# A decoder trunk on one core: three converted weight buffers and six raw ones in place of two and seven

## The chip, the cores and the metric

The kernel runs on one core of one Trainium2 chip. Its time is device microseconds (us) of one execution; the time of a kernel is the median over its runs. A core has TensorE (PE in the profile; PEld are its weight loads, which run beside the matmuls), VectorE (DVE), ScalarE (ACT) and GpSimd (POOL), each with a queue of its own that is worked off in order, and SyncE (SP), which here only issues DMAs.

## The reference

Two layers over 272 tokens (16 meta tokens and 256 of the sequence). Each layer mixes tokens (an RG-LRU group and an attention group side by side) and then adds PEER, a retrieval over 16384 experts of one neuron each:

```python
def peer(h, wq, subkeys, u, v):
    q = (h @ wq).reshape(B, T, PEER_HEADS, 2, D_SUBKEY)
    s = jnp.einsum('bthpd,pkd->bthpk', q, subkeys)
    top_s, top_i = lax.top_k(s, PEER_TOPK)
    ...
    gates = jax.nn.softmax(best_s, axis=-1)
    def one_chunk(args):
        hc, ec, gc = args
        act = gelu(einsum('cd,ckd->ck', hc, take(u, ec)))
        return einsum('ck,ckd->cd', gc * act, take(v, ec))

def reference(...):
    for l in range(2):
        z = rms_norm(h, mix_norm_g[l]) @ w_in[l]
        ...
        h = h + mixed @ w_out[l]
        h = h + peer(rms_norm(h, ffn_norm_g[l]), peer_wq[l], peer_subkeys[l], peer_u[l], peer_v[l])
    return h[:, N_META:]
```

## The kernel before

Most tokens do not gather their experts. For 224 tokens in layer 0 and 208 in layer 1 the kernel multiplies with all 16384 rows of `u`, applies the gelu, multiplies with a dense matrix of gates (zero but for the chosen experts) and multiplies with all rows of `v`. The other tokens fetch their rows one by one: a *gather* is one indirect DMA of 128 rows (512 KB), and a layer has 96.

All weights are fp32 and come as *blocks* of 128x1024 (512 KB). The list `order` fixes their sequence, per layer 14 of `w_in`, 8 of `w_out`, 16 of `wq`, 128 of `uT` (the u stage), 128 of `v` (the v stage), with the gathers put in between: 17 and 32 in the u stages of the two layers, 79 and 64 in the v stages. In the v stage of layer 1 one gather comes after every second block. Block loads are issued by SP (L147), gathers by POOL (L1067).

A load goes into one of the PF buffers of the pool `raw`, blocks and gathers in turn, so that load n reuses the buffer of load n-PF. Since TensorE multiplies in fp16, each block is split into a high half, `hi` (ScalarE, L216), and a rest, `lo` (VectorE, L217); `hi` and `lo` have two buffers each, which come free when TensorE has used them. A block is then 24 matmuls: 16 with `hi`, then 8 with `lo` (`mm3`, and L1142 for `v`). `block(kind, l, b)` is called before a block's matmuls: it has `conv` emit the split of the block after it, and the steps of the gathers in between. A gather is not split; VectorE works on it in the raw buffer (L1050 for `u`, a dot product; L1052 and L1054 for `v`, the sum `acc`), which frees the buffer.

In the v stage the activations are split as well, for two blocks at a time (`wsplit`): ScalarE writes the high part of `ww` (L1129), VectorE the rest (L1130). `ww` has two such pair buffers, and a pair is split one pair ahead.

In the `wq` and u stages VectorE also has the selection of the experts (top-k, one-hots, gates), which generators emit piece by piece between blocks. What stands where in an engine's queue is decided by a scheduler from the order of emission, from what is free by its own reckoning, and from a priority that the split has (`PRI`).

Of the kernel before, what the change touches and what calls it, by code (L numbers as in the profile page):

```python
# [10 lines left out]
F16 = mybir.dt.float16  # L11
# [15 lines left out]
NK = 128  # L27
# [19 lines left out]
NSP = (32, 48)  # L47
NU = (2, 2)
UB = (((64, 127, 16), (116, 124, 1)), ((60, 127, 32),))
PF = 7  # L50
ATT = ((3, 7), (1, 7))
LRU_AT = (1, 2, 3, 4)
LRU_FIRST = 0
# [88 lines left out]
def trunk(tc, a, out, dbg=None):  # L142
# [15 lines left out]
    with ExitStack() as ctx:  # L158
        per = ctx.enter_context(tc.tile_pool(name="per", bufs=1))
        raw_p = ctx.enter_context(tc.tile_pool(name="raw", bufs=PF))  # L160
        hl_p = ctx.enter_context(tc.tile_pool(name="hl", bufs=2))
        psp = ctx.enter_context(tc.tile_pool(name="psp", bufs=2, space=PSUM))
        PB = {"u": 2, "g": 2, "v": 4}

        def ps(tag):
            return psp.tile([128, 512], F32, name="ps_" + tag, tag=tag, bufs=PB[tag])
# [26 lines left out]
        def issue(n):  # L193
            while st["dma"] < min(n, len(order)):
                w, l, b = order[st["dma"]]
                t = raw_p.tile([128, D], F32, name="raw", tag="raw")
                if w == "gather":
                    hook["load"](t, *b)
                else:
                    dma(t, a[w][l, b])  # L200
                raws[st["dma"]] = t
                st["dma"] += 1

        def conv(n):
            while st["conv"] < min(n, len(order)):
                k = st["conv"]
                issue(k + PF)
                r = raws.pop(k)
                st["conv"] += 1
                if order[k][0] == "gather":  # L210
                    hook["step"](r, *order[k][2])
                    continue
                hi = hl_p.tile([128, D], F16, name="hi", tag="hi")
                lo = hl_p.tile([128, D], F16, name="lo", tag="lo")
                with tc.high_priority(offset=PRI):
                    A.activation(hi, r, AF.Copy, scale=WS)  # L216
                    V.scalar_tensor_tensor(out=lo, in0=r, scalar=WS, in1=hi, op0=ALU.mult, op1=ALU.subtract)  # L217
                hls[k] = (hi, lo)

        def ahead(k, n):  # L220
            while n:
                k += 1
                if k < len(order) and order[k][0] != "gather":
                    n -= 1
                elif k >= len(order):
                    break
            return k

        def block(kind, l, b):
            k = st["k"]  # L230
            while order[k][0] == "gather":
                k += 1
            assert order[k] == (kind, l, b), (order[k], kind, l, b)
            st["k"] = k + 1
            conv(ahead(k, 1) + 1)
            return hls.pop(k)

        def mm3(o, w, xhi, xlo, first=True, n=8, off=0):
# [19 lines left out]
        def area(tag, dt, shape=None, name=None):  # L258
            return per.tile(shape or [128, 8, T], dt, name=name or tag, tag=tag)
# [54 lines left out]
        def mixing(l, col, hh, hl, sq):  # L314
            SQ_H = [(one, sq[:, c]) for c in range(8)]
            C0 = NM if l else 0
            with tc.tile_pool(name="mix", bufs=1) as mp:
# [51 lines left out]
                def w_in(b):  # L369
                    w = block("w_in", l, b)  # L370
                    c0 = C0 if b >= 7 else 0
                    o = ps("v")[:, c0:T]
                    mm3(o, w, hh[:, :, c0:], hl[:, :, c0:])
                    return o
# [256 lines left out]
                def w_out_half(b, half, then=None):  # L631
                    w = block("w_out", l, 4 * half + b)
                    for m in range(2):
                        o = ps("u" if half else "v")[:, C0:T]
                        mm3(o, w, mh[:, 4 * half:, C0:], ml[:, 4 * half:, C0:], n=4, off=4 * m)
                        V.scalar_tensor_tensor(out=hT[:, 2 * b + m, C0:], in0=o, scalar=1.0 / WS, in1=hT[:, 2 * b + m, C0:], op0=ALU.mult, op1=ALU.add)
                        if then:
                            then(2 * b + m)
                        yield
# [112 lines left out]
                for b in range(4):  # L752
                    for _ in w_out_half(b, 1, then):
                        pass
                w = block("wq", l, 0)
                o = ps("v")[:, C0:T]
                mm3(o, w, hh[:, :, C0:], hl[:, :, C0:])
# [61 lines left out]
        def peer(l, col, hh, hl, rs, wq0):  # L819
            with tc.tile_pool(name="peer", bufs=1) as pp:  # L820
                SD = S - NSP[l]
# [9 lines left out]
                def al(shape, dt):  # L831
                    n = int(np.prod(shape))
                    e = n // 2 if dt == F16 else n
                    r = flata[:, cur[0]:cur[0] + e]
                    cur[0] += (e + 7) // 8 * 8
                    assert cur[0] <= cur_end[0]
                    if dt != F32:
                        r = r.bitcast(dt)
                    if len(shape) == 1:
                        return r  # L840
                    nm = "abcd"[:len(shape)]
                    return r.rearrange("p (%s) -> p %s" % (" ".join(nm), " ".join(nm)), **{nm[i]: shape[i] for i in range(len(shape) - 1)})
# [17 lines left out]
                hn = al([2, T], F32)  # L860
# [261 lines left out]
                    pump(PUMP[1] - prog["t"] / 960.0)  # L1122
                drain()
                pv = [ps("v") for _ in range(4)]
                ww = area("hn", F16, [128, 2, 2, 2, SD], "ww")

                def wsplit(j):
                    b = j // 2 % 2
                    A.activation(ww[:, b, 0], act[:, j:j + 2], AF.Copy)  # L1129
                    V.tensor_tensor(out=ww[:, b, 1], in0=act[:, j:j + 2], in1=ww[:, b, 0], op=ALU.subtract)  # L1130

                wsplit(0)
                for j in range(NK):
                    hi, lo = block("v", l, j)
                    if j % 2 and j + 1 < NK:
                        wsplit(j + 1)
                    wh, wl = ww[:, j // 2 % 2, 0, j % 2], ww[:, j // 2 % 2, 1, j % 2]

                    def mv(c, k):
                        o = pv[c // 2][:, (c % 2) * SD:(c % 2) * SD + SD]  # L1140
                        s = slice(c * 128, c * 128 + 128)
                        P.matmul(o, (hi, hi, lo)[k][:, s], (wh, wl, wh)[k], start=j == 0 and k == 0 and c % 2 == 0, stop=j == NK - 1 and k == 2, skip_group_check=True)  # L1142

                    if j < NK - 1:
                        for k in range(3):
                            for c in range(8):
                                mv(c, k)
                    else:
                        for c in range(8):
                            for k in range(3):  # L1150
                                mv(c, k)
                return pv

        if True:
# [12 lines left out]
            hh, hl = hx[:, 0], hx[:, 1]  # L1167
# [4 lines left out]
            for l in range(L):  # L1172
                hh, hl, rs, wq0 = mixing(l, cols[l], hh, hl, sq)
                if dbg is not None:
                    dma(dbg["h%d" % l], hT)
                pv = peer(l, cols[l], hh, hl, rs, wq0)
                if l + 1 < L:
                    hx, sq = area("gx", F16, [128, 2, 8, T], "hgx"), area("gy", F32)
                    hh, hl = hx[:, 0], hx[:, 1]
                for c in range(8):  # L1180
                    sd = S - NSP[l]
                    hd = hT[:, c, NM:NM + sd]
                    V.scalar_tensor_tensor(out=hd, in0=pv[c // 2][:, (c % 2) * sd:(c % 2) * sd + sd], scalar=1.0 / WS, in1=hd, op0=ALU.mult, op1=ALU.add)  # L1183
                    if l + 1 < L:
                        hsplit(c, cols[l + 1][:, C_MIX + c:C_MIX + c + 1], hh, hl, sq)
                    elif c % 2:
                        dma(out[:, c - 1:c + 1], hT[:, c - 1:c + 1, NM:T])


def build(arrays, dbg=False):  # L1190
    import concourse.bacc as bacc
    nc = bacc.Bacc("TRN2", target_bir_lowering=False, num_devices=1)
    aps = {k: nc.dram_tensor(k, v.shape, F32, kind="ExternalInput").ap() for k, v in arrays.items()}
    out = nc.dram_tensor("outT", (128, 8, S), F32, kind="ExternalOutput").ap()
    d = {"h%d" % l: nc.dram_tensor("h%d" % l, (128, 8, T), F32, kind="ExternalOutput").ap() for l in range(L)} if dbg else None
    with tile.TileContext(nc) as tc:
        trunk(tc, aps, out, d)
    return nc
# [9 lines left out]
```

## Time and profile before

| | |
|---|---|
| time, median of 3 runs | 1669.47 us (1664.43 to 1669.9) |
| the profiled execution | 1668.44 us, span 1666.7 us |
| PE busy | 1588.0 us, 95% of the span |
| PEld busy | 1467.8 us, 88% |
| DVE busy | 1503.8 us, 90% |
| ACT busy | 1098.2 us, 66% |
| POOL busy | 320.6 us, 19% |
| from HBM | 417.46 MB, 253 GB/s in the mean of all traffic |
| granted clock of TensorE | 0.993 of full speed |

The span is what the rows lie in; the execution's own time is 1.7 us longer. Matmuls overlap in the records, so a gap between them (idle time with its releaser in brackets) tells more than the busy share. DMA share is the mean busy share of the 16 DMA engines.

### The profile page before, as it was taken

The page shows a single profiled execution, that of the slowest core. Times are in us where ns is not written, and L with a number is a line of the kernel's source. Part 1 is how long each engine was busy: PE and PEld are TensorE (multiplying, and loading weights), DVE is VectorE, ACT ScalarE, POOL GpSimd, SP SyncE. Part 2 cuts the span into 40 slices and gives each one's busy share as a digit, 9 for nine tenths or more (in the row PEclk, how much of TensorE's full clock was granted, in tenths as well). Part 3 has the DMA queues.
Part 4 walks back from the last instruction along what each step waited for, and adds up shares of the span by engine and source line. Part 5 has one row for each costly group of instructions (what it writes and reads, how often), then busy time and mean ns, then how long its engine had stood idle before and what let it go on. Part 6 is the DMA issues. An engine that isn't in the chain of part 4 may idle for free.

```text
span 1666.7 us, 40245 instructions
## 1 busy us (share of the span) xinstructions
PE 1588.0 (95%) x15926; PEld 1467.8 (88%) x15926; DVE 1503.8 (90%) x3074; ACT 1098.2 (66%) x2001; POOL 320.6 (19%) x256
## 2 busy tenths in 40 slices
PE   9989999999999999999999899899999999999997
PEld 6667798899999999999967687789988899999997
DVE  6889989889999999988978899997999998989886
ACT  6857565789987555555557565678988755555653
POOL 1000000101102333333210000002124124353253
PEclk9999999999999999999999999999999999999999
DMA  7305465667777999999973054567787899999995
GB/s 291 114 11 169 141 208 198 216 204 235 246 257 254 339 374 360 367 358 352 359 260 119 3 178 140 201 217 237 229 278 272 279 351 333 346 353 353 365 338 203
DMA packets 117709, 421.21 MB, mean 253 GB/s; under 512 B 14416, under 2 KB 15824, under 8 KB 117008
## 3 DMA queue, kind: packets, MB, share of 16 engines
q1 hardware_dynamic: 88592, 317.88, 54.2%
q0 software_dynamic: 28928, 100.76, 17.4%
q8 instruction: 124, 2.03, 0.5%
q14 instruction: 65, 0.53, 0.1%
HBM read 417.46 MB, written 1.05 MB: 251 GB/s over the span
## 4 chain that ended last, share of the span: by engine, by line
PE 40%; DVE 14%; DMA 5%; ACT 3%; issue 3%; POOL 1%; DVEq 0%; POOLq 0%; ACTq 0%
PE ps_v L1142 26%; DVE lo L217 6%; PE ps_u L246 3%; DMA raw<-v,act 3%; PE ps_u L242 3%; PE ps_u L243 3%; ACT hi L216 1%; PE ps_g L966 1%; DMA raw<-v 1%; POOL raw L1067 1%; DVE act L767 1%; DVE act L764 1%; PE ps_v L243 1%; PE ps_v L242 1%; PE ps_v L246 1%
## 5 line engine op out<-in xcount | busy, mean ns | idle before, releaser
L216 ACT ACTIVATE hi<-raw 128x1024 f16<-128x1024 f32 x588 | 619.8, 1055 | 430.8 <-PE ps_v L1142 208.6
L217 DVE SCALAR_TENSOR_TENSOR lo<-raw,hi 128x1024 f16<-128x1024 f32 x588 | 710.6, 1218 | 71.2 <-ACT hi L216 64.0
L1142 PE MATMUL ps_v<-ww,hi 128*128 128x224 f16 (+1 forms) x4096 | 426.8, 257 | 11.0 <-DVE ww L1130 10.1
L242 PE MATMUL ps_u<-hn,hi 128*128 128x224 f16 (+2 forms) x2112 | 413.1, 257 | 8.2 <-ACT hi L216 6.8
L243 PE MATMUL ps_u<-hn,hi 128*128 128x224 f16 (+2 forms) x2112 | 413.0, 256 | 0.0
L1142 PEld LDWEIGHTS <-hi 128*128 128x128 f16 x4096 | 382.5, 98 | 13.6 <-issue 12.5
L246 PEld LDWEIGHTS <-lo 128*128 128x128 f16 x2656 | 244.1, 98 | 54.0 <-DVE lo L217 43.2
L242 PEld LDWEIGHTS <-hi 128*128 128x128 f16 x2656 | 260.0, 98 | 27.5 <-ACT hi L216 11.5
L243 PEld LDWEIGHTS <-hi 128*128 128x128 f16 x2656 | 259.9, 98 | 14.8 <-issue 4.5
L246 PE MATMUL ps_u<-hn,lo 128*128 128x224 f16 (+2 forms) x2112 | 242.0, 257 | 25.4 <-DVE lo L217 24.7
L1142 PE MATMUL ps_v<-ww,lo 128*128 128x224 f16 (+1 forms) x2048 | 235.7, 257 | 5.4 <-DVE lo L217 5.0
L1067 POOL DMA_INDIRECT raw<-ur,act x96 | 131.2, 1367 | 467.6 <-DVE lo L217 237.4
L1067 POOL DMA_INDIRECT raw<-v,act x96 | 157.8, 1644 | 248.1 <-DVE lo L217 186.4
L1142 PEld LDWEIGHTS <-lo 128*128 128x128 f16 x2048 | 190.5, 98 | 10.8 <-DVE lo L217 10.0
L957 ACT ACTIVATE ohb<-oha,gl 128x128 f16<-128x128 f16 x432 | 138.7, 396 | 13.2 <-DVE oha L952 13.2
L1054 DVE SCALAR_TENSOR_TENSOR acc<-raw,act,acc 128x1024 f32<-128x1024 f32 x90 | 115.1, 1279 | 28.9 <-DMA raw<-v,act 28.8
L922 POOL DMA_DIRECT2D act<-comb x40 | 20.4, 518 | 599.0 <-DVE oha L952 310.6
L243 PE MATMUL ps_v<-hgx,hi 128*128 128x272 f16 (+1 forms) x480 | 113.6, 277 | 0.4 <-DVE hgx L311 0.4
L242 PE MATMUL ps_v<-hgx,hi 128*128 128x272 f16 (+1 forms) x480 | 113.3, 277 | 0.4 <-DVE hT L1183 0.3
L1050 DVE SCALAR_TENSOR_TENSOR raw<-raw,act 128x1024 f32<-128x1024 f32 x64 | 77.6, 1216 | 5.6 <-DMA raw<-ur,act 4.6
L1130 DVE TENSOR_TENSOR ww<-act,ww 128x448 f16<-128x448 f32 (+1 forms) x128 | 76.8, 600 | 0.0
L1129 ACT ACTIVATE ww<-act 128x448 f16<-128x448 f32 (+1 forms) x128 | 69.8, 547 | 0.0
(304 smaller groups left out, 1611.1 us busy)
## 6 DMA issues: line engine op xcount, KB each, us to landing
raw<-uT SPq DMA_DIRECT2D x256, 512.0 KB, 4.3
raw<-v SPq DMA_DIRECT2D x256, 512.0 KB, 6.2
raw<-wq SPq DMA_DIRECT2D x32, 512.0 KB, 3.3
raw<-w_in SPq DMA_DIRECT2D x28, 512.0 KB, 6.8
raw<-w_out SPq DMA_DIRECT2D x16, 512.0 KB, 3.3
uq<-uq SPq DMA_DIRECT2D x2, 1152.0 KB, 10.1
ukv<-ukv SPq DMA_DIRECT2D x2, 1024.0 KB, 8.2
raw<-ur,act POOLq DMA_INDIRECT x96, 6.5
```

Of the source, the lines that this page charges most:

```text
L216: A.activation(hi, r, AF.Copy, scale=WS)
L217: V.scalar_tensor_tensor(out=lo, in0=r, scalar=WS, in1=hi, op0=ALU.mult, op1=ALU.subtract)
L242: P.matmul(o, hi[:, s], xhi[:, c], start=first and c == 0, stop=False, skip_group_check=True)
L243: P.matmul(o, hi[:, s], xlo[:, c], start=False, stop=False, skip_group_check=True)
L246: P.matmul(o, lo[:, s], xhi[:, c], start=False, stop=c == n - 1, skip_group_check=True)
L957: A.activation(ob[:, 1, t], oe[:, t], AF.Copy, scale=gl[:, b * 8 + t:b * 8 + t + 1])
L1050: keep = V.scalar_tensor_tensor(out=t, in0=t, scalar=1.0, in1=hr, op0=ALU.mult, op1=ALU.mult, accum_out=dot[:, s:s + 1])
L1054: keep = V.scalar_tensor_tensor(out=acc, in0=t, scalar=dot[:, s:s + 1], in1=acc, op0=ALU.mult, op1=ALU.add)
L1067: G.indirect_dma_start(out=t, out_offset=None, in_=tab, in_offset=bass.IndirectOffsetOnAxis(ap=ei[g][:, s:s + 1], axis=0))
L1129: A.activation(ww[:, b, 0], act[:, j:j + 2], AF.Copy)
L1130: V.tensor_tensor(out=ww[:, b, 1], in0=act[:, j:j + 2], in1=ww[:, b, 0], op=ALU.subtract)
L1142: P.matmul(o, (hi, hi, lo)[k][:, s], (wh, wl, wh)[k], start=j == 0 and k == 0 and c % 2 == 0, stop=j == NK - 1 and k == 2, skip_group_chec ...
```

## The change

The pool `raw` gets six buffers in place of seven and `hi` and `lo` three each in place of two. `block` has the split emitted two blocks ahead in place of one, and with it the gather steps on the way. `ww` gets four pair buffers in place of two, and a pair of activations is split two pairs ahead; the first two pairs are split before the loop. The amount of work is the same, and so is the memory of the weight buffers (7 + 2 and 6 + 3 times 4 KB in a partition). `ww` lies in a tile that is larger than it in both kernels.

```diff
--- before.py
+++ after.py
@@ -47,7 +47,8 @@
 NSP = (32, 48)
 NU = (2, 2)
 UB = (((64, 127, 16), (116, 124, 1)), ((60, 127, 32),))
-PF = 7
+PF = 6
+NHL = 3
 ATT = ((3, 7), (1, 7))
 LRU_AT = (1, 2, 3, 4)
 LRU_FIRST = 0
@@ -158,7 +159,7 @@
     with ExitStack() as ctx:
         per = ctx.enter_context(tc.tile_pool(name="per", bufs=1))
         raw_p = ctx.enter_context(tc.tile_pool(name="raw", bufs=PF))
-        hl_p = ctx.enter_context(tc.tile_pool(name="hl", bufs=2))
+        hl_p = ctx.enter_context(tc.tile_pool(name="hl", bufs=NHL))
         psp = ctx.enter_context(tc.tile_pool(name="psp", bufs=2, space=PSUM))
         PB = {"u": 2, "g": 2, "v": 4}
 
@@ -232,7 +233,7 @@
                 k += 1
             assert order[k] == (kind, l, b), (order[k], kind, l, b)
             st["k"] = k + 1
-            conv(ahead(k, 1) + 1)
+            conv(ahead(k, NHL - 1) + 1)
             return hls.pop(k)
 
         def mm3(o, w, xhi, xlo, first=True, n=8, off=0):
@@ -1122,19 +1123,20 @@
                     pump(PUMP[1] - prog["t"] / 960.0)
                 drain()
                 pv = [ps("v") for _ in range(4)]
-                ww = area("hn", F16, [128, 2, 2, 2, SD], "ww")
+                ww = area("hn", F16, [128, 4, 2, 2, SD], "ww")
 
                 def wsplit(j):
-                    b = j // 2 % 2
+                    b = j // 2 % 4
                     A.activation(ww[:, b, 0], act[:, j:j + 2], AF.Copy)
                     V.tensor_tensor(out=ww[:, b, 1], in0=act[:, j:j + 2], in1=ww[:, b, 0], op=ALU.subtract)
 
                 wsplit(0)
+                wsplit(2)
                 for j in range(NK):
                     hi, lo = block("v", l, j)
-                    if j % 2 and j + 1 < NK:
-                        wsplit(j + 1)
-                    wh, wl = ww[:, j // 2 % 2, 0, j % 2], ww[:, j // 2 % 2, 1, j % 2]
+                    if j % 2 and j + 3 < NK:
+                        wsplit(j + 3)
+                    wh, wl = ww[:, j // 2 % 4, 0, j % 2], ww[:, j // 2 % 4, 1, j % 2]
 
                     def mv(c, k):
                         o = pv[c // 2][:, (c % 2) * SD:(c % 2) * SD + SD]
```

The scheduler moves instructions on VectorE in two places that matter below. The first is the u stage of layer 1, around the end of the top-k work: `MAX`, `MAX_INDEX` and `MATCH_REPLACE` are its last rounds and `CAST` the first step of what follows. Before, from the `lo` of block 26 to that of block 27:

```order
L217 SCALAR_TENSOR_TENSOR lo<-raw,hi 128x1024
L767 MAX_INDEX act<-act 128x8
L763 MAX_INDEX act<-act 128x8
L764 MATCH_REPLACE act<-act 128x112
L781 CAST act<-act 128x256
L766 MAX act<-act 128x8
L767 MAX_INDEX act<-act 128x8
L217 SCALAR_TENSOR_TENSOR lo<-raw,hi 128x1024
```

And now, from the `lo` of block 27 to that of block 28 (lines after L50 are one higher):

```order
L218 SCALAR_TENSOR_TENSOR lo<-raw,hi 128x1024
L768 MAX_INDEX act<-act 128x8
L764 MAX_INDEX act<-act 128x8
L765 MATCH_REPLACE act<-act 128x112
L782 CAST act<-act 128x256
L767 MAX act<-act 128x8
L768 MAX_INDEX act<-act 128x8
L218 SCALAR_TENSOR_TENSOR lo<-raw,hi 128x1024
```

The step that stood between the `lo` of blocks 26 and 27 now stands between those of blocks 27 and 28: a `lo` has some of the other work behind it that it had ahead.

The second is the v stage of layer 1, blocks 112 to 116 (`acc` is the sum over gathered rows, which waits for the gather's landing). Before, from the `lo` of blocks 112 and 113 on:

```order
L217 SCALAR_TENSOR_TENSOR lo<-raw,hi 128x1024 x2
L1054 SCALAR_TENSOR_TENSOR acc_19603<-raw,act,acc_19603 128x1024
L1130 TENSOR_TENSOR ww<-act,ww 128x416
L217 SCALAR_TENSOR_TENSOR lo<-raw,hi 128x1024 x2
L1054 SCALAR_TENSOR_TENSOR acc_19603<-raw,act,acc_19603 128x1024
```

And now, from the same stretch on:

```order
L218 SCALAR_TENSOR_TENSOR lo<-raw,hi 128x1024 x2
L1131 TENSOR_TENSOR ww<-act,ww 128x416
L1055 SCALAR_TENSOR_TENSOR acc_19576<-raw,act,acc_19576 128x1024
L218 SCALAR_TENSOR_TENSOR lo<-raw,hi 128x1024 x2
L1131 TENSOR_TENSOR ww<-act,ww 128x416
```

Before, a pair is `lo` of an even block, `lo` of the odd one, `acc`, `ww`. Now it is `lo` of an odd block, `lo` of the even one after it, `ww`, `acc`; `ww` stands ahead of the wait for the gather, and belongs to a later pair. POOL's queue holds the same instructions in the same order as before. On SP only the start of layer 1 differs, by one load of `w_in`.

## Rows read from the trace of the kernel before

**Rows 1.** The page: part 4, the chain by line, and a group of part 5.
```profile
PE ps_v L1142 26%; DVE lo L217 6%; PE ps_u L246 3%; DMA raw<-v,act 3%; PE ps_u L242 3%; PE ps_u L243 3%; ACT hi L216 1%; PE ps_g L966 1%; DMA raw<-v 1%; POOL raw L1067 1%; DVE act L767 1%; DVE act L764 1%; PE ps_v L243 1%; PE ps_v L242 1%; PE ps_v L246 1%
...
L216 ACT ACTIVATE hi<-raw 128x1024 f16<-128x1024 f32 x588 | 619.8, 1055 | 430.8 <-PE ps_v L1142 208.6
```

**Rows 2.** Windows by stage: stretch, its length, busy us (instructions) of engines, PEclk, DMA share, GB/s.
```profile
194.00:320.00 126.00, 115.01 (x1139) 106.75 (x1138) 120.69 (x403) 81.78 (x109) 2.54 (x5) 1.00 0.58 194
...
537.00:846.00 309.00, 304.30 (x3130) 300.62 (x3129) 279.23 (x325) 166.45 (x198) 97.40 (x85) 0.99 0.96 357
1027.00:1120.00 93.00, 80.24 (x846) 73.81 (x844) 92.92 (x312) 58.94 (x69) 0.00 (x0) 1.00 0.59 198
1120.00:1200.00 80.00, 79.28 (x925) 77.66 (x923) 67.89 (x103) 71.29 (x171) 17.47 (x29) 1.00 0.70 227
1200.00:1340.00 140.00, 129.63 (x1517) 124.07 (x1515) 139.55 (x211) 109.43 (x272) 38.03 (x25) 1.00 0.83 278
...
1362.00:1664.00 302.00, 287.39 (x3137) 282.06 (x3134) 259.25 (x285) 163.91 (x195) 120.53 (x62) 0.99 0.91 330
```

**Rows 3.** Waits of TensorE's weight loads, whole run: us, times, longest.
```profile
PEld L246 <- DVE lo L217: 43.2, 70, 1.9
```

**Rows 4.** One saturated stretch of uT blocks in layer 1: timeline, 1047 to 1052 us.
```profile
1047.15 1.22 DVE L217 SCALAR_TENSOR_TENSOR lo<-raw,hi 128x1024 f16<-128x1024 f32 x1
...
1049.81 1.22 DVE L217 SCALAR_TENSOR_TENSOR lo<-raw,hi 128x1024 f16<-128x1024 f32 x1
...
1051.08 0.65 PEld L246 LDWEIGHTS <-lo 128*128 128x128 f16 x8 [0.58 <-DVE lo L217]
```

**Rows 5.** Waits in the v stage of layer 1, 1362 to 1664 us.
```profile
DVE acc L1054 <- DMA raw<-v,act: 21.5, 11, 4.1
...
PEld L1142 <- issue: 11.3, 8, 2.8
PE ps_v L1142 <- DVE ww L1130: 9.6, 6, 2.6
...
PEld L1142 <- DVE lo L217: 4.6, 10, 0.5
```

**Rows 6.** One of these waits: timeline, 1630.5 to 1637 us.
```profile
1632.21 1.28 DVE L1054 SCALAR_TENSOR_TENSOR acc<-raw,act,acc 128x1024 f32<-128x1024 f32 x1 [4.05 <-DMA raw<-v,act]
1633.41 0.58 DVE L1130 TENSOR_TENSOR ww<-act,ww 128x416 f16<-128x416 f32 x1
...
1633.91 2.35 DVE L217 SCALAR_TENSOR_TENSOR lo<-raw,hi 128x1024 f16<-128x1024 f32 x2
1634.05 0.88 PE L1142 MATMUL ps_v<-ww,hi 128*128 128x208 f16 x8 [2.60 <-DVE ww L1130]
...
1635.18 0.65 PEld L1142 LDWEIGHTS <-lo 128*128 128x128 f16 x8 [0.50 <-DVE lo L217]
...
1636.54 4.52 POOL L1067 DMA_INDIRECT raw<-v,act  x1 [6.29 <-DVE lo L217]
```

**Rows 7.** A block's pace in that stage: timeline of weight loads, 1588 to 1592 us.
```profile
1589.00 1.44 PEld L1142 LDWEIGHTS <-hi 128*128 128x128 f16 x16
...
1591.14 0.90 PEld L1142 LDWEIGHTS <-hi 128*128 128x128 f16 x10
```

**Rows 8.** Line L1067, the gathers, 1362 to 1664 us: ns min/median/max, then landing.
```profile
L1067 POOL DMA_INDIRECT raw<-v,act x46: 947/1748/4522, 1361.0 to 1641.4; - x46
...
DMA to landing us min/median/max: 4.8/7.9/11.6
```

**Rows 9.** VectorE by line and shape, 1362 to 1664 us.
```profile
L217 DVE SCALAR_TENSOR_TENSOR lo<-raw,hi 128x1024 f16<-128x1024 f32 x128 | 153.4, 1219 | 14.9 <-ACT hi L216 13.0 <-PE ps_g L1028 1.4
L1054 DVE SCALAR_TENSOR_TENSOR acc<-raw,act,acc 128x1024 f32<-128x1024 f32 x45 | 57.6, 1279 | 21.7 <-DMA raw<-v,act 21.5
L1130 DVE TENSOR_TENSOR ww<-act,ww 128x416 f16<-128x416 f32 x64 | 37.3, 583 | 0.0
```

**Rows 10.** Waits in the v stage of layer 0, 537 to 846 us.
```profile
PEld L1142 <- DVE lo L217: 5.4, 9, 1.3
```

## Prediction

> **What bounds the kernel now.** I read the page first, then a table of windows by stage, then the waits of each stage, then timelines of single waits.
>
> The chain on the page lies mostly on TensorE, and the only other line that holds much of it is VectorE's `lo`, 6% of the span [rows 1]. The windows tell where that comes from [rows 2]. In three stretches of the `wq` and u stages (194 to 320, 1027 to 1120 and 1200 to 1340 us) VectorE is busy for 96%, 100% and 100% of the time, and TensorE is not. Between two of them, from 1120 to 1200, it is the other way round: VectorE has 12.1 us to spare (80 less 67.89) and TensorE none. The v stages look different: there VectorE has 10% and 14% to spare, and the DMA engines have almost nothing (share 0.96 and, with the run-out at the end, 0.91).
>
> So there are two kinds of wait. In the u stage the weight loads of the `lo` matmuls wait for VectorE, 43.2 us in 70 waits, none over 1.9 [rows 3]. Such a place is in [rows 4]: two `lo` start 2.66 us apart, 1.22 of that is the `lo` itself, so 1.44 us of other work stands between them, and a TensorE block is shorter than this. VectorE idles nowhere; TensorE follows its pace.
>
> In the v stage of layer 1 TensorE's weight loads lose 11.3 us in 8 waits and 4.6 in 10 [rows 5]. One of the long ones is in [rows 6]. VectorE reaches `acc` and stands 4.05 us, until a gather has landed; behind it in the queue stand `ww` and two `lo`; TensorE waits 2.60 us for `ww` and 0.50 for the `lo`. So VectorE may stand about 0.95 us (4.05 less 3.10) before TensorE pays. In all VectorE stands 21.5 us at `acc`, 11 times [rows 5].
>
> **The change, part by part.** No operation is added; buffers and places in queues change. Where rows give no price I bound it.
>
> *Three `hi`/`lo` buffers in the saturated stretches.* Where VectorE never idles, one more buffer makes no work disappear. What it gives is a lead, once for each stretch: a `lo` stands ahead of other work that stood ahead of it, as the first pair of listings shows, by at most the work between two `lo`, 1.44 us [rows 4]. Three stretches give 3 x 1.44 = 4.3 us. The lower end is nothing (the lead is used up before the stretch begins), the upper the whole 43.2 us. I stay at 4.3, since [rows 2] show busy time that has to go somewhere, and it doesn't shrink.
>
> *`ww` two pairs ahead, `lo` one block ahead, in the v stage.* Behind `acc` now stands `lo` alone, and it is for a later block. A block takes 2.14 us [rows 7]. Counted from the end of the block that frees the buffer of the `lo` just ahead, VectorE reaches `acc` after `hi` 1.06, `lo` 1.22 and `ww` 0.58, at 2.9 us [rows 1, 9]. The `lo` behind it is needed three blocks and 16 of 24 matmuls later, at 3.67 x 2.14 = 7.85. Less 1.28 for `acc` and 1.22 for `lo` this leaves 5.35, so VectorE may stand 2.45 us in place of 0.95.
>
> *Six raw buffers.* The price of this lies with the gathers. In the v stage of layer 1 the sequence is two blocks and a gather. With seven buffers a gather takes the buffer of a block, and is issued as soon as that block's `lo` is done, four blocks before VectorE wants it: 8.56 us, less 0.28 from release to issue (1633.91 + 2.35 to 1636.54 in [rows 6]), is 8.3. With six buffers, two whole rounds of the sequence, a gather always takes a gather's buffer, and is issued when the `acc` of the gather two before is done: 8.56 - 1.28 - 0.28 = 7.0 us. The median from issue to landing is 7.9 [rows 8]. So at today's latency VectorE would stand at most gathers, and two slots would set the stage's pace: (7.9 + 1.28 + 0.28) / 2 = 4.73 us for two blocks. That is the pace of today: 302 us over 64 pairs is 4.72 [rows 2]. TensorE alone would need 4.28. Latency should fall somewhat, since one load fewer is in flight: of 7.9 us, 1.75 are POOL's writing of the descriptors [rows 8], the other 6.2 are spent behind up to six other loads; a seventh of it would be 0.9 us, which would just bring 4.28. The DMA engines are near full in either case, so I take 0.2 us of the 0.9: 64 x 0.2 / 2 = 6.4 us gained. The ends are 0 and 64 x 0.45 = 28.8 (TensorE's pace).
>
> On whether POOL gets slower there are rows too: writing descriptors takes 0.947 to 4.522 us [rows 8], and the slow one in [rows 6] runs beside two `lo` that follow each other without a gap. [...]
>
> *The v stage of layer 0.* The same, but with 1.62 loads for a block the sequence doesn't fit six buffers, so no gather waits for gathers alone. There are 5.4 us of waits, none over 1.3 [rows 10], and the DMA share is 0.96 [rows 2]. The ends are 5.4 gained and as much lost; I take 1 gained.
>
> *Block loads.* A block's load is issued when the `lo` six or seven items back is done, and that waits for a `hi` buffer which TensorE frees three or two blocks back. One goes against the other, so loads are issued at the same place of TensorE's program as before: nothing.
>
> *Mixing and the start of layers.* One split more stands ahead of the chains there, 1.06 us on ScalarE and 1.22 on VectorE [rows 1, 9]; it is taken from where it stood later. Nothing, with 2 us to either side.
>
> *Sum.* 4.3 + 6.4 + 1 = 11.7 us off the profiled 1668.4 (its median over the runs is 1.0 higher): 1656.7, and 1658 as a median.
>
> **The rivals.**
> *The gathers set the pace and get slower (slower).* The place is the v stage of layer 1, the mechanism the two slots. If latency rises over 2 x 4.72 - 1.56 = 7.88 us, the stage is longer than today. For it: 7.9 is already there, and gathers written in 4.52 us exist. Should one in six more be written in 4.52 in place of 1.75, the mean rises by 0.46, a pair takes 4.96, and the stage 64 x 0.24 = 15.4 us more; with the 4.3 of the u stage that is 1679.5, as a median 1681. [...]
> *Nothing comes of it.* The lead is eaten before the saturated stretches begin, latency stays: 1668, a median of 1669. For it: VectorE's and the DMA engines' full windows.
> *The waits mostly go.* Half of the 43.2 us, because the waits come from bunches of work and not from its sum, and the 15.9 us of the v stage of layer 1 [rows 3, 5]: 1668.4 - 37.5 = 1631, a median of 1632. For it: 12.1 us of VectorE's time idle in between; against it, three windows at 96 to 100%.
>
> **The numbers.** A forecast like mine (1648 to 1664): 0.46. Mostly gone: 0.08. Nothing, or gains and losses that cancel (1664 to 1674): 0.24. Slower by the gathers: 0.22. A measurement tells some 0.3% from no change, 5 us; so faster 0.54, same 0.24, slower 0.22. The range leaves out most of the 0.08 below and half of the 0.22 above: 1644 to 1684.
>
> **What would show it.** Right: in the v stage of layer 1 POOL waits for `acc` more than for `lo`; the waits for `ww` are gone; VectorE's wait at `acc` comes often and short, and TensorE loses less than the 15.9 us of now; loads of the u stage's `lo` still wait over 35 us with VectorE still full. Wrong: these waits fall by half (then it was bunching), or the v stage of layer 1 takes longer than 302 us and landings a median over 7.9 (then the slots decide). What would make the forecast wrong without touching its steps is another order of work in the mixing, where I priced nothing.

## The result, and the profile after

The changed kernel takes 1905.6 us (median of 4 runs, 1900.68 to 1908.84) against 1669.7 for the one before: 1.141 times as long, 95% interval 1.1365 to 1.1456. The forecast was a median of 1658. The profiled execution has a span of 1901.5 us, 234.8 more than before.

Laid side by side by the starts of the `lo`s, the two traces differ by stage like this: up to layer 0's v stage the changed kernel gains 8.1 us; in that stage (367.0 in place of 308.8) it loses 58.2; in layer 1's mixing it gains 1.2, in its `wq` and u stages it loses 10.6; in layer 1's v stage (469.5 in place of 296.6, counted to the last block's `lo`) it loses 172.9. So the two v stages hold nearly the whole loss. Windows of them, after, with the columns of [rows 2]:

```profile
527.00:894.00 367.00, 320.41 (x3137) 307.00 (x3135) 280.16 (x334) 166.54 (x199) 129.97 (x86) 0.95 0.84 300
1421.00:1890.00 469.00, 330.32 (x3063) 305.55 (x3062) 257.13 (x277) 165.13 (x195) 108.74 (x62) 0.88 0.62 212
```

VectorE has the same 257 us of work in layer 1's stage as before, but now it idles for 212. The DMA engines, near full before (0.91), are busy 62%. Nothing is saturated: engines wait for each other. The waits of this stage (compare [rows 5]; `...` stands for lines left out):

```profile
POOL raw L1068 <- DVE acc L1055: 214.9, 35, 8.2
ACT hi L217 <- DVE lo L218: 179.6, 49, 5.8
PEld L1144 <- DVE lo L218: 145.2, 51, 5.0
DVE acc L1055 <- DMA raw<-v,act: 144.3, 38, 6.3
...
POOL raw L1068 <- DVE raw L1051: 73.7, 12, 8.5
DVE raw L1051 <- DMA raw<-ur,act: 53.1, 14, 6.1
POOL raw L1068 <- DVE lo L218: 41.4, 9, 7.4
...
DVE lo L218 <- ACT hi L217: 6.0, 5, 2.9
...
DVE acc L1053 <- DMA raw<-v,act: 3.1, 1, 3.1
```

Read as a circle: VectorE stands 200.5 us at gather steps (L1051, L1053, L1055) for data; with its work and the 6.0 us that it waits for `hi` this fills 464 of the 469 us, so VectorE's queue sets the stage. POOL, which issues the gathers, stands for VectorE to free the buffer; TensorE stands for the `lo`s queued behind VectorE's wait. Before, VectorE stood 24.4 us in this stretch, counted the same way. In the timeline (compare [rows 6]) the circle is one gather long:

```profile
1699.56 1.23 DVE L1051 SCALAR_TENSOR_TENSOR raw<-raw,hr 128x1024 f32<-128x1024 f32 x1 [3.47 <-DMA raw<-ur,act]
...
1700.71 2.36 DVE L218 SCALAR_TENSOR_TENSOR lo<-raw,hi 128x1024 f16<-128x1024 f32 x2
1701.07 1.69 POOL L1068 DMA_INDIRECT raw<-ur,act  x1 [5.78 <-DVE raw L1051]
...
1701.99 0.89 PE L1144 MATMUL ps_v<-ww,lo 128*128 128x208 f16 x8 [1.36 <-DVE lo L218]
...
1704.34 1.06 ACT L217 ACTIVATE hi<-raw 128x1024 f16<-128x1024 f32 x1 [0.83 <-PE ps_v L1144]
...
1706.65 1.23 DVE L1051 SCALAR_TENSOR_TENSOR raw<-raw,hr 128x1024 f32<-128x1024 f32 x1 [3.08 <-DMA raw<-ur,act]
...
1707.81 2.36 DVE L218 SCALAR_TENSOR_TENSOR lo<-raw,hi 128x1024 f16<-128x1024 f32 x2
1708.16 1.69 POOL L1068 DMA_INDIRECT raw<-ur,act  x1 [5.40 <-DVE raw L1051]
1709.08 1.00 PEld L1144 LDWEIGHTS <-lo 128*128 128x128 f16 x7 [2.88 <-DVE lo L218]
```

A step ends at 1700.79, the next gather is issued 0.28 us later, lands at 1706.6, and the very next gather step waits for it. Only then are two `lo`s let through, at 1707.81, for blocks whose `hi` was written by 1705.4. In 47 of 63 cases a gather is issued after the end of the step just before its own; in the kernel before in none. Landing itself got shorter ([rows 8]: 7.9 in the median), with the DMA engines busy 62%:

```profile
L1068 POOL DMA_INDIRECT raw<-v,act x46: 947/1687/4521, 1422.1 to 1871.7; - x46
...
DMA to landing us min/median/max: 5.2/6.0/9.1
```

In the u stages the waits of [rows 3] fell by more than half, and in layer 0's v stage those of [rows 10] rose ninefold. After, whole run and 527 to 894 us:

```profile
PEld L247 <- DVE lo L218: 18.3, 30, 1.9
```

```profile
PEld L1144 <- DVE lo L218: 47.8, 26, 5.7
```

### The profile page after: what moved, and what is told of

It reads as the page before. It is cut to its first block, busy times and chain, and to the rows that moved or that the text cites. A ratio compares the mean times of both kernels' runs of the same rounds, so it can differ in the third digit from the quotient of the medians.

```text
span 1901.5 us, 40247 instructions
## 1 busy us (share of the span) xinstructions
PE 1651.9 (87%) x15926; PEld 1512.5 (80%) x15926; DVE 1504.6 (79%) x3074; ACT 1096.7 (58%) x2001; POOL 340.4 (18%) x256
## 5 line engine op out<-in xcount | busy, mean ns | idle before, releaser
L1144 PE MATMUL ps_v<-ww,hi 128*128 128x224 f16 (+1 forms) x4096 | 459.1, 269 | 7.1 <-ACT ww L1130 6.0
L243 PE MATMUL ps_u<-hn,hi 128*128 128x224 f16 (+2 forms) x2112 | 418.1, 258 | 6.9 <-ACT act L1118 2.9
L1144 PEld LDWEIGHTS <-hi 128*128 128x128 f16 x4096 | 405.9, 103 | 19.5 <-issue 7.0
L244 PE MATMUL ps_u<-hn,hi 128*128 128x224 f16 (+2 forms) x2112 | 418.3, 258 | 0.0
L1144 PE MATMUL ps_v<-ww,lo 128*128 128x224 f16 (+1 forms) x2048 | 257.4, 273 | 174.4 <-DVE lo L218 174.4
L1144 PEld LDWEIGHTS <-lo 128*128 128x128 f16 x2048 | 199.2, 104 | 199.9 <-DVE lo L218 193.0
L243 PEld LDWEIGHTS <-hi 128*128 128x128 f16 x2656 | 261.5, 98 | 22.2 <-issue 7.3
L244 PEld LDWEIGHTS <-hi 128*128 128x128 f16 x2656 | 261.7, 99 | 19.1 <-issue 8.1
L247 PEld LDWEIGHTS <-lo 128*128 128x128 f16 x2656 | 248.8, 98 | 29.1 <-DVE lo L218 18.3
L1055 DVE SCALAR_TENSOR_TENSOR acc<-raw,act,acc 128x1024 f32<-128x1024 f32 x90 | 115.5, 1283 | 182.2 <-DMA raw<-v,act 182.0
L1068 POOL DMA_INDIRECT raw<-v,act x96 | 169.8, 1769 | 389.2 <-DVE acc L1055 248.2
L1068 POOL DMA_INDIRECT raw<-ur,act x96 | 139.1, 1449 | 532.1 <-DVE lo L218 200.1
L1051 DVE SCALAR_TENSOR_TENSOR raw<-raw,hr 128x1024 f32<-128x1024 f32 x32 | 39.1, 1223 | 78.7 <-DMA raw<-ur,act 78.7
L1051 DVE SCALAR_TENSOR_TENSOR raw<-raw,act 128x1024 f32<-128x1024 f32 x64 | 77.9, 1217 | 17.7 <-DMA raw<-ur,act 16.6
```

The source lines that it names most:

```text
L243: P.matmul(o, hi[:, s], xhi[:, c], start=first and c == 0, stop=False, skip_group_check=True)
L244: P.matmul(o, hi[:, s], xlo[:, c], start=False, stop=False, skip_group_check=True)
L247: P.matmul(o, lo[:, s], xhi[:, c], start=False, stop=c == n - 1, skip_group_check=True)
L1051: keep = V.scalar_tensor_tensor(out=t, in0=t, scalar=1.0, in1=hr, op0=ALU.mult, op1=ALU.mult, accum_out=dot[:, s:s + 1])
L1055: keep = V.scalar_tensor_tensor(out=acc, in0=t, scalar=dot[:, s:s + 1], in1=acc, op0=ALU.mult, op1=ALU.add)
L1068: G.indirect_dma_start(out=t, out_offset=None, in_=tab, in_offset=bass.IndirectOffsetOnAxis(ap=ei[g][:, s:s + 1], axis=0))
```

## The experiments

A number that the built kernels give, with no time in it, turned out to order most of them: the **lead** of a load, counted in entries of VectorE's queue (`lo`s and gather steps) from the last use of the buffer that the load takes to the load's own use. It is counted from the places that the raw tiles have in memory and from the order of VectorE's instructions. Two things set it: which buffer the pool hands out (the one that its own reckoning frees first, not always the one of the load PF before), and how far the scheduler moves a gather step forward. The table has the mean lead of the gathers (in brackets the least), the length of the stage, and how long VectorE stands at gathers in it, in one profiled execution of each kernel.

| kernel | layer 0: lead | stage us | stands | layer 1: lead | stage us | stands |
|---|---|---|---|---|---|---|
| before | 6.7 (6) | 308.8 | 13.2 | 7.0 (7) | 296.6 | 24.4 |
| changed | 5.5 (3) | 367.0 | 80.9 | 3.4 (2) | 469.5 | 200.5 |
| 1: ww two | 5.8 (5) | 339.2 | 49.0 | 5.1 (5) | 338.1 | 69.1 |
| 2: lead one | 5.3 (2) | 371.1 | 87.9 | 6.1 (6) | 310.4 | 43.4 |
| 3: two for gathers | 5.2 (3) | 368.7 | 78.5 | 5.9 (4) | 317.8 | 55.3 |
| 4: before, one for gathers | 2.6 (1) | 423.2 | 145.8 | 3.0 (3) | 424.9 | 154.2 |
| 5: before, six | 5.7 (5) | 348.7 | 53.7 | 6.0 (6) | 301.0 | 25.0 |
| 6: changed, seven | 6.4 (3) | 344.7 | 59.1 | 4.3 (3) | 338.9 | 73.7 |
| 7: before, eight | 7.7 (7) | 304.0 | 0.0 | 8.0 (8) | 279.8 | 0.2 |
| 8: before, ww four | 6.3 (2) | 350.5 | 48.1 | 7.0 (7) | 295.1 | 23.3 |
| 9: three and three, ww two | 7.8 (7) | 369.1 | 0.0 | 8.9 (7) | 350.3 | 0.0 |
| 10: seven, ww two | 6.8 (6) | 309.8 | 19.4 | 6.1 (6) | 321.9 | 57.0 |
| 11: before, three and four | 7.8 (6) | 307.3 | 1.0 | 9.0 (7) | 286.7 | 0.0 |
| 12: three and four, ww two | 7.8 (7) | 302.6 | 0.7 | 8.9 (7) | 296.5 | 0.0 |

The order has exceptions. In layer 0 the mean hides a few short leads (runs 6 and 8, down to 3 and 2). In layer 1 run 10 is slower than run 5 with the same lead, and run 4 is faster than the changed kernel with a shorter one. In runs 9, 11 and 12 VectorE hardly stands at gathers, and something else sets the stage.

The first four runs were to tell apart three theories named in the first text.

**1. The activation split put back**, in the changed kernel:

```diff
-                ww = area("hn", F16, [128, 4, 2, 2, SD], "ww")
+                ww = area("hn", F16, [128, 2, 2, 2, SD], "ww")
...
-                    if j % 2 and j + 3 < NK:
-                        wsplit(j + 3)
+                    if j % 2 and j + 1 < NK:
+                        wsplit(j + 1)
```

> The changed kernel with the activation split as before: two pair buffers of ww, one pair ahead; six raw and three hi/lo buffers stay. Where the built programs place the raw tiles, 62 of the 64 gathers of layer 1's v stage then take a block's buffer, as before the change (changed kernel: 47 take the buffer of the gather just before). Theory A (in the changed kernel nearly all gathers go through one buffer, each issued only when VectorE is done with the one before): v stage of layer 1 back to 295 to 310 us; the stage of layer 0, where 36 of 79 gathers take the buffer of the gather two before, 300 to 340; total 1650 to 1700. Theory B (VectorE stands at a gather that was put two ahead of the lo's of its place): here gathers stand one ahead as before, so also about 1660 to 1700; this run does not tell A from B. Theory C (six raw buffers hold too few loads in flight, whatever the order): still 1880 to 1910.

Measured: 1745.3 us, ratio 1.046 (1.039 to 1.053). Two thirds of the loss are gone with `ww` alone, but layer 1's stage is not back: 338.1. All three theories missed the total.

**2. The weights split one block ahead again**, in the changed kernel:

```diff
-            conv(ahead(k, NHL - 1) + 1)
+            conv(ahead(k, 1) + 1)
```

> The changed kernel with the split of weights one block ahead again; six raw buffers, three hi/lo buffers and four pair buffers of ww stay. By the placement of the tiles 59 of 64 gathers of layer 1's v stage take the buffer of the gather two before: the ring of two slots that the prediction reckoned with. Theory A: pace (6.0 to 7.9 landing + 1.28 + 0.28) / 2 = 3.8 to 4.7 us per pair, TensorE's 4.28 or the loads set it; stage 275 to 305 us; total 1650 to 1700. Theory B: gathers stand one ahead of their place, as before: also 1660 to 1700. Theory C: 1880 to 1910.

Measured: 1751.1 us, 1.049 (1.042 to 1.056). Layer 1's 310.4 us (4.85 per pair) lies 5 above theory A's bounds, but A's formula holds with the landing measured here: a median of 8.1, so (8.1 + 1.56) / 2 = 4.83. Layer 0's 371.1 none had priced, and all three missed the total.

**3. Two raw buffers for gathers, four for blocks**, in the changed kernel (NG is 2):

```diff
-        raw_p = ctx.enter_context(tc.tile_pool(name="raw", bufs=PF))
+        raw_p = ctx.enter_context(tc.tile_pool(name="raw", bufs=PF - NG))
+        gat_p = ctx.enter_context(tc.tile_pool(name="gat", bufs=NG))
...
+                if w == "gather":
+                    t = gat_p.tile([128, D], F32, name="gat", tag="gat")
```

> The changed kernel with the six raw buffers parted: two that only gathers use, four that only blocks use. VectorE's queue in the v stage of layer 1 stays as in the changed kernel, each gather two ahead of the lo's of its place. Theory A: two slots, pace 3.8 to 4.7 us per pair of blocks in layer 1, so 280 to 310 us; in layer 0 79 gathers at 3.8 to 4.7 take 300 to 371; total 1650 to 1740. Theory B: VectorE still stands at gathers with lo's behind, layer 1's stage stays over 420 us, total over 1820. Theory C: four buffers for blocks are fewer still: 1880 or more.

Measured: 1751.5 us, 1.047 (1.040 to 1.054). Layer 1's stage is 151.7 us shorter than in the changed kernel, although gather steps stand as far forward in VectorE's queue: theory B in its plain form falls. A's bounds are missed too, by 8 us in layer 1 and 12 in the total.

**4. One raw buffer for gathers, six for blocks**, in the kernel before (the same edit, NG is 1):

> The kernel before, its seven raw buffers parted: one that only gathers use, six that only blocks use. Nothing else; no gather stands ahead of its place in VectorE's queue. Theory A: one gather at a time, 1.28 for its use, 0.3 to the issue and 5.2 to 6.5 landing: 6.8 to 8.1 us each; v stage of layer 1 435 to 520 us in place of 302, of layer 0 540 to 640 in place of 309; total 2030 to 2250. Theory B: gathers in their place cost as before, or less: 1660 to 1700. Theory C: as many buffers in all as before, 1660 to 1700.

Measured: 2064.1 us (one run). Here every step stands in its place, each gather waits for the one before, and A alone expected the total. The v stages came out under A's bounds (423.2 and 424.9 us): in layer 1 a gather took 424.9 / 64 = 6.64 us, which less 1.28 for its use and 0.28 to the issue leaves some 5.1 for its landing (A had 5.2 to 6.5), and in layer 0 gathers that were left ran on into the mixing. The waits of layer 1's stage show the circle of the changed kernel:

```profile
POOL gat L1072 <- DVE acc L1059: 241.9, 44, 6.4
DVE acc L1059 <- DMA gat<-v,act: 109.5, 44, 4.1
```

So gathers whose issue waits for the step just before cost 128.3 us in layer 1 here; the changed kernel, where 47 of them do, lost 172.9, with landings of 6.0 in place of some 5.1. Layer 0, and what layer 1 lost in run 1, stayed open. The next four runs took the change's parts one by one from the kernel before, and gave the changed kernel its seventh buffer back.

**5. Six raw buffers alone**, in the kernel before:

```diff
-PF = 7
+PF = 6
```

> The kernel before with six raw buffers in place of seven, nothing else; gathers stand in their place in VectorE's queue, and 60 of 64 in layer 1's v stage take the buffer of the gather two before. Theory C (a raw buffer is taken about 10 us for each load, from issue to the end of its use, whatever the number of buffers; with six a load comes every 9.6 to 10.4 / 6 = 1.60 to 1.73 us): layer 0's v stage, 207 loads, 331 to 358 us in place of 309; layer 1's 305 to 320 as in the run with the lead of one; total 1700 to 1740. Theory H (the third hi/lo buffer and the two blocks of lead cost the time, since VectorE meets gathers earlier): six raw buffers alone cost little, 1665 to 1685.

Measured: 1717.3 us, 1.027 (1.021 to 1.034). Layer 0's stage is inside C's bounds, layer 1's 301.0 below them. Theory H's total is missed.

**6. The changed kernel with seven** (PF = 7; room from tiles that share memory):

> The changed kernel with seven raw buffers, the room for it won by letting small tiles share memory (the selector rows of the mixing lie in a buffer used later, the gate scratch in the gelu scratch, four tables are cut to the tokens used). Gathers stand one to two ahead of their place as in the changed kernel, but 60 of 64 in layer 1's v stage take a block's buffer. Theories A and C: the v stages back to 300 to 315 and 290 to 310 us, the 8 us won up to layer 0's v stage stay; total 1650 to 1672. Theory H (the order on VectorE): layer 1's stage 330 us or more, total 1695 or more.

Measured: 1755.5 us, 1.049 (1.042 to 1.056). Theories A and C fall as they were put: 60 of 64 gathers take a block's buffer, there are seven, and layer 1's stage still takes 338.9 us. What these gathers share with those of runs 1 to 4 is a lead shorter than the 7.0 of the kernel before, here 4.3 entries: the block whose buffer they take was itself worked on late. Theory H was right on the number; run 3 had shown that order alone isn't it. From here on the theory is the lead (L in the texts).

**7. Eight raw buffers**, in the kernel before (PF = 8, room as in run 6):

> The kernel before with eight raw buffers (room as in the run before). Theory C: a load could come every 10.2 / 8 = 1.28 us, TensorE is the bound then: VectorE's 21.5 us at gathers in layer 1 shrink, that stage 287 to 297 us, layer 0's 303 to 309; total 1650 to 1663. Rival (seven buffers are enough, the DMA engines set the pace of the v stages): 1664 to 1672.

Measured: 1646.1 us, 0.983 (0.977 to 0.990), the fastest kernel of the study, by more than C's 1650 to 1663. VectorE does not stand at gathers, and TensorE is busy almost throughout both stages:

```profile
534.00:838.00 304.00, 302.65 (x3131) 301.36 (x3129) 278.19 (x323) 166.90 (x197) 114.48 (x85) 0.99 0.98 363
1355.00:1635.00 280.00, 278.57 (x3109) 278.03 (x3107) 258.77 (x277) 163.96 (x196) 102.75 (x61) 1.00 0.96 352
```

**8. Only `ww` with four pair buffers**, in the kernel before (the change's last hunk, seven raw and two `hi`/`lo` buffers):

> The kernel before with four pair buffers of ww and the activations split two pairs ahead, nothing else (seven raw, two hi/lo buffers). The prediction's step on ww: TensorE's 9.6 us of waits for ww in layer 1 go, VectorE may stand longer at gathers; total 1658 to 1667. Rival (the placement changes: in layer 0's v stage 21 gathers in place of 8 take the buffer of a gather two or three before, and are issued late): layer 0's stage 5 to 20 us longer, total 1670 to 1690.

Measured: 1709.8 us, 1.021 (1.014 to 1.027). The rival was right on the place and too low on the size: layer 0's stage is 41.7 us longer. There 21 gathers have leads under 6, down to 2, where none had before. Waits, 533 to 883 us:

```profile
PEld L1144 <- DVE lo L218: 41.2, 21, 5.0
...
DVE raw L1051 <- DMA raw<-ur,act: 30.4, 10, 7.8
```

The last four runs put the lead itself to the test, in both directions.

**9. Six buffers, three for gathers and three for blocks, `ww` two** (the edits of runs 1 and 3, NG is 3):

> The changed kernel with the activation split as before (two pair buffers of ww) and the six raw buffers parted, three for gathers, three for blocks. The lead of a load is counted in entries of VectorE's queue (lo's and gather steps) between the last use of the buffer that it takes and its own use. Gathers have 7.8 in layer 0 and 8.9 in layer 1, none under 7 (with the six shared: 5.8 and 5.1); blocks have 4.9 and 4.5 (6.1 and 6.4). Theory L (the lead of the gathers decides; at 7 entries the stages took 309 and 297 us, at 8 entries 304 and 280): stages 304 to 312 and 280 to 297, total 1640 to 1668, although there are six buffers in all. Theory C (six are too few): 1700 to 1745. Theory T (blocks are late when they have 4.5 to 4.9 entries, 7 us): TensorE waits for loads of blocks, 1690 or more.

Measured: 1795.1 us, 1.074 (1.067 to 1.080). As L says, VectorE does not stand at gathers at all, but L's stages and total are missed, since theory T is right: blocks with 4.5 to 4.9 entries are late, and ScalarE and VectorE wait for them. Layer 1's stage:

```profile
ACT hi L222 <- DMA raw<-v: 140.7, 75, 4.8
DVE lo L223 <- ACT hi L222: 91.7, 58, 4.4
```

**10. Seven raw, three `hi`/`lo`, `ww` two** (run 6 with the edit of run 1):

> The changed kernel with seven raw buffers and the activation split as before; three hi/lo buffers and two blocks of lead stay. Gathers have a lead of 6 to 8 entries in layer 0 (mean 6.75; kernel before 6.69) and 6.1 in layer 1 (7.0). Theory L: stages 305 to 315 and 298 to 312 us, the 6 to 8 us won before them stay; total 1655 to 1675. Theory H (meeting gathers earlier because weights are split two blocks ahead is what costs, however long their lead): as the run with seven and three, 1740 or more.

Measured: 1702.5 us, 1.016 (1.008 to 1.024). Layer 0's stage is back with its lead (309.8). Layer 1's, 321.9, and the total are above L's bounds: the stage has the lead of run 5 (6.1 and 6.0) and takes 20.9 us more. One difference stands in the length of POOL's `DMA_INDIRECT` for the gathers, of run 5 first and then of run 10:

```profile
L1067 POOL DMA_INDIRECT raw<-v,act x46: 947/1053/1414, 1402.8 to 1687.0; - x46
```

```profile
L1070 POOL DMA_INDIRECT raw<-v,act x46: 947/1687/5932, 1372.8 to 1676.8; - x46
```

In both a gather is issued when `acc` ends. In run 5 VectorE goes on with `ww` (0.58 us in [rows 9]), in run 10 with two `lo`s (1.22 each there), and POOL's `DMA_INDIRECT` takes 0.63 us longer in the median. On a ring of two gathers that would be 0.32 for a pair of blocks, 20.3 us over 64 pairs. That this is the whole reason is not shown. Run 2 has the same lead and a `DMA_INDIRECT` as long, and its stage takes 310.4 us, only 9.4 more than run 5's:

```profile
L1068 POOL DMA_INDIRECT raw<-v,act x46: 947/1686/3326, 1424.7 to 1722.9; - x46
```

In runs 5 and 10 the longer `DMA_INDIRECT` (1.687 us against 1.053) goes with the longer VectorE instruction after `acc` (1.22 against 0.58). That the one makes the other longer no run shows.

**11. Three buffers for gathers and four for blocks**, in the kernel before (the edit of run 3, NG is 3):

> The kernel before, its seven raw buffers parted, three for gathers and four for blocks; nothing else, no more memory. Gathers have a lead of 7.8 and 9.0 entries (6.7 and 7.0 when shared), blocks 6.5 and 6.0 (7.2 and 7.0). Theory L: VectorE hardly stands at gathers; stages 303 to 309 and 278 to 290 us as with eight shared buffers; total 1642 to 1660. Theory T (blocks at 6 entries are late, with two hi/lo buffers): 1675 or more.

Measured: 1666.1 us, 0.997 (0.994 to 1.0005). VectorE stands no more, and both stages are inside L's bounds, but the total is above them, and the medians don't tell it from no change. The profiled execution, 10 us shorter in the span, was the fastest of its ten, so its stages flatter the kernel. Whether blocks (6.0 entries in layer 1) gave back what gathers won is not shown.

**12. All of it with long leads: three `hi`/`lo`, `ww` two, seven raw as three and four** (runs 10 and 3):

> Three hi/lo buffers, weights split two blocks ahead, two pair buffers of ww, seven raw buffers parted into three for gathers and four for blocks. Leads: gathers 7.8 and 8.9, none under 7; blocks 6.5 and 6.0, with a third hi/lo buffer behind them. Theory L: stages 303 to 308 and 276 to 288 us, 6 to 8 us won before layer 0's v stage; total 1632 to 1650. If the third hi/lo buffer has no worth beside VectorE's full windows, it equals the run before.

Measured: 1670.7 us, 1.002 (0.998 to 1.006), not the 1632 to 1650 expected, and no better than run 11. So L missed the total in all four runs; what it got right is that VectorE stops standing at gathers when their lead is long. The third `hi`/`lo` buffer bought nothing measurable here. Why layer 1's stage takes 296.5 us with VectorE never standing at a gather, where eight shared buffers take 279.8, is not settled. Its blocks have 6.0 entries against 8.0, but those of run 11 have 6.0 too, and its stage takes 286.7.

## Why the prediction was wrong, point by point

**Six raw buffers, layer 1: the step that failed.** The prediction has a gather "issued when the `acc` of the gather two before is done", 7.0 us ahead of its use. It took the buffers in turn (the text ahead of it has load n reuse the buffer of load n-PF) and VectorE's queue in the order of the program. With both nearly as it assumed, its two slots give the right pace: in run 5, six buffers alone, the stage takes 301.0 us, 4.70 per pair against the 4.73 that it had for an unchanged landing (its forecast was 0.1 less, by its estimate that landings get 0.2 us shorter with one load fewer in flight, which no run shows apart). In the changed kernel neither holds. The longer leads of the splits let the scheduler put gather steps one to two gathers further forward, the pool then frees a gather's buffer first and hands it to the next gather (47 of 64 take the buffer of the gather just before), and the lead is 3.4 entries. An entry is 296.6 / 192 = 1.545 us, so a lead of n leaves (n - 1) x 1.545 - 0.28 us for landing: 9.0 us at 7, 7.4 at 6, 2.8 at 3. The landings' medians are 7.9 at 7 (before), 8.1 and 8.4 at 6 (runs 2 and 10) and 6.0 in the changed kernel. Two slots were one. Run 3 shows what that cost: with the gather steps as far forward and two buffers kept for gathers, 151.7 of the 172.9 us are gone. The listing of blocks 112 to 116 showed `acc` moved behind `ww`, but not by how many gathers, since its names carried no order of the blocks.

**Six raw buffers, layer 0.** The prediction had "no gather waits for gathers alone", so 1 us gained, 5.4 either way: it lost 58.2. The reason given was beside the point. It doesn't matter whose buffer a gather takes, but how late that buffer's last use stands in the queue. An entry is 308.8 / 207 = 1.49 us; a lead of 6 leaves 7.2, which is the landing's median in this stage before (4.6/7.2/9.7), 5 leaves 5.7. Run 5, order unchanged, puts 26 of 77 gathers at 5 and costs 39.9.

**Block loads at nothing.** Right for the changed kernel as far as VectorE goes. Its blocks have leads of 6.3 and 7.3, and though ScalarE waits 107.1 us for them in layer 0, VectorE waits only 2.9 and 6.0 us for `hi` in the two v stages (16.2 and 13.0 before). Run 9 shows where it ends: at 4.5 to 4.9 entries the stages take 369 and 350 us with no gather late. By the leads, that is the asymmetry which the prediction missed: for a block the third `hi`/`lo` buffer makes up for the lost raw one; a gather has none.

**`ww` two pairs ahead.** The waits for VectorE's `ww` went, as said. That VectorE may stand longer was worth little where it could be seen: in run 8, `ww` alone, layer 1 gains 1.5 us, less than executions differ by. The full 2.45 us, with `lo` a block further ahead, no run shows apart. Unpriced was what it does to the order: with four pair buffers gather steps stand further forward, and layer 0 loses 41.7. That is read from the built order; why the scheduler does so was not tried.

**Three `hi`/`lo` buffers, saturated stretches.** 4.3 us gained was the estimate. In layer 0's `wq` and u stages 2.1 were gained, in layer 1's 10.6 lost, although the waits for `lo` fell from 43.2 to 18.3, the sign given for bunching. In layer 1 part of the time went into other waits of TensorE, for the products of the gates (1.3 and 0.7 us before):

```profile
PEld L967 <- issue: 14.4, 12, 2.2
PE ps_g L967 <- ACT act L979: 12.6, 11, 2.0
```

**Mixing at nothing, 2 us either side.** Layer 0 gained 6.0 up to `wq`, layer 1 gained 1.2.

**The rivals.** "The gathers set the pace" had the place and the sign, but not the mechanism: it asked for landings over 7.88 us, and they fell to 6.0. Its price, 15.4, was less than a tenth of layer 1's loss, because it too counted two slots. Nor did POOL's `DMA_INDIRECT`, which that rival takes for the writing, get longer: 1.687 us in the median, 1.748 before [rows 8]; the traces give its length, not what POOL does in it. (The two `lo` that [rows 6] show end at 1636.26, before the slow one begins at 1636.54; beside it VectorE ran the next `acc` and `ww` and two more `lo`s.) Of the signs, "POOL waits for `acc` more than for `lo`" came (214.9 against 41.4), as did the end of the waits for `ww`; "TensorE loses less" did not. Of the signs of being wrong, the longer stage came, the longer landing did not.

## What to carry to other kernels

When a pool is shared by transfers with different consumers, count for each kind how many entries of the in-order consumer's queue lie between the last use of its buffer and its own use, in the built order and placement, and hold that times the pace against the landing. Deeper buffering further down (a split two ahead, more pair buffers) can shorten that count without touching the pool (in run 8 from 6.7 to 6.3 in the mean of layer 0, the least from 6 to 2). Prices, from one execution of each kernel: with the blocks in time, each microsecond that VectorE stood at gathers made a stage 0.7 to 1.0 us longer than in run 7, wherever it stood 25 us or more.

## What the runs showed of the hardware

TensorE's clock fell. In layer 1's v stage its granted clock is 0.88 of full speed, before 0.99, and TensorE is busy 330.32 us for 3063 records, before 287.39 for 3137 [rows 2]. After some of the waits it goes on at 0.50 of full speed, as from 1710 to 1712 us below. Windows of 2 us (columns as above, PEclk third from the end), and TensorE's timeline there:

```profile
1706.00:1708.00 2.00, 0.45 (x5) 0.20 (x3) 1.34 (x3) 0.00 (x0) 0.00 (x0) 1.00 0.64 242
1708.00:1710.00 2.00, 0.92 (x6) 0.81 (x7) 2.00 (x2) 0.89 (x1) 1.69 (x1) 0.73 0.00 0
1710.00:1712.00 2.00, 2.00 (x13) 1.74 (x12) 0.66 (x2) 0.71 (x2) 0.00 (x0) 0.50 0.94 309
1712.00:1714.00 2.00, 2.00 (x23) 1.95 (x21) 0.00 (x0) 1.00 (x1) 0.00 (x0) 0.92 0.94 293
```

```profile
1709.08 1.57 PE L1144 MATMUL ps_v<-ww,lo 128*128 128x208 f16 x8 [2.64 <-DVE lo L218]
1710.44 2.52 PE L1144 MATMUL ps_v<-ww,hi 128*128 128x208 f16 x16
1712.80 0.88 PE L1144 MATMUL ps_v<-ww,lo 128*128 128x208 f16 x8
1713.51 1.59 PE L1144 MATMUL ps_v<-ww,hi 128*128 128x208 f16 x16
```

After a wait of 2.64 us the first block takes 0.69 + 0.93 = 1.6 us more than the next; after the wait of 1.36 at 1701.99 it does not (0.89 for eight). The length of the wait alone does not decide: in this stage a wait of 2.76 us at 1501.69 was followed by eight matmuls in 0.89, and from there to 1506 the granted clock is 1.00; in the kernel before a wait of 2.60 us at 1634.05 was followed by eight in 0.88 [rows 6]. What decides, no run shows.

That the slow blocks lengthen the stage is not shown. VectorE's queue sets it, VectorE waits 6.0 us for `hi` in it and 200.5 for gathers, and among the engines that POOL stood for before a gather TensorE is not.
